# Layer 0's modulation: from reductions on VectorE to float32 products on TensorE in four groups of the array's columns

## The chip, the cores and the metric

The kernel runs on one core of one Trainium2 chip. Its time is the device time of one execution in microseconds (us), as the median of several runs. The engines are PE (TensorE), DVE (VectorE), ACT (ScalarE), POOL (GpSimd) and SP (SyncE, which here issues nearly every DMA, in one queue and in order). PEld is PE's weight load, the part of a matmul that sets the stationary operand. Each engine takes its instructions in the order in which the program has them, so an instruction that waits holds up all that stand behind it on its engine.

## The reference

Two blocks follow each other. The first takes 512 tokens of width 1024 through a gated delta rule and a dilated attention, both fed by projections of the normed input, and a gated feed-forward network. The second has two layers with a stream of 512 tokens and one of 256 context tokens; layer 0 has the "even" mixer (neighbourhood attention and differential attention), layer 1 the "odd" one (grouped attention and a long convolution, the filter of which comes from a small network with sines). Each layer of the second block is modulated:

```python
for layer in range(DEPTH_2):
    mod_l = (silu(c) @ w_ada[layer] + b_ada[layer])[:, None, :]
    mod_c = silu(c_ctx) @ w_ada[layer] + b_ada[layer]
    sh1_l, sc1_l, g1_l, sh2_l, sc2_l, g2_l = split(mod_l, 6, axis=-1)
    ...
    h_l = modulate(x_l, sh1_l, sc1_l)        # rms_norm(x) * (1 + scale) + shift
    h_c = modulate(x_c, sh1_c, sc1_c)
    ...                                      # mixer, then the same with sh2, sc2, g2 for the feed-forward
```

c and c_ctx are single vectors of 1024; w_ada[layer] is 1024 x 6144 in float32 (24 MB). So a layer's modulation is two vectors times one matrix, 2 x 6144 numbers, and each weight is used twice. It does not depend on x: it can be computed at any time before its use. The first third (shift and scale of the mixer's input) is wanted when layer 0 begins, the rest when the mixer's output is added and in the feed-forward.

## The kernel before

**Matmuls in three products.** The big projections take their weights in 512 KB chunks (`wchunk`, L305 to L315). A chunk is loaded to `wraw` by SP (two buffers), ACT rounds it to `whi` (L311), POOL takes the difference `wlo` (L312); there are three buffers of each. Activations are split in the same way, and `mm3` (L321) adds three products: hi by hi, hi by lo, lo by hi (L323, L324, L325). A matmul that is not written so, with plain float32 operands, takes PE two instruction records.

**The order.** The program is written as straight Python; a scheduler fixes at compile time the order of the instructions on each engine, with its own model of how long each takes. `issue_after` forces an instruction behind another one.

**Stage A, from the start to 130 us: projections of the delta rule.** Chunks of `w_qkv` feed PE; DVE scales each product tile (`cv_x`, L535), ACT copies it with a tap of the short convolution (`cv_y`, L537), DVE adds the other taps, ACT and DVE form the SiLU (`cv_t`). ACT also makes `whi`, in the same queue.

**Stage B, from 130.7 to 228.8 us: dilated attention's projections.** Eight chunks of `w_qk` (192 matmuls, `dq`, `dk`) and four of `w_v` (96 matmuls, `dv`, L890). In between PE runs small float32 products of the filter's network (`hyena_mlp`, L1867: `fz`, `fh` by `fw`), each followed by a sine made of six DVE instructions (`fn`, `fa`), and the row of biases (`oh`, `rl`, L868). Then the recurrence and the attention begin with transposes (`ps_p`, `ps_a`).

**Stage C, from 896.0 to 1137.7 us: layer 0's in-projection.** 24 chunks of `we_in`: six jobs of four chunks, each job 512 output columns for six tiles of 128 tokens (4 of x, 2 of the context), 144 matmuls a job, 864 in all. A job holds six PSUM banks, three called `ps_m` and three `ps_mx`, until its last chunk. For the jobs of queries and keys ACT squares and copies each tile (`qk_sq` L1364, `qk_raw` L1365, which frees the bank), DVE sums the squares (`qk_ssq` L1366), then DVE and POOL norm and rotate (L1389 to L1401), and PE transposes the result (`ps_t`, L1414) among the next job's matmuls. Stage C ends with the first scores (`ps_s`, L1571).

**The modulation.** `ada` (L1074) works on DVE. It loads both vectors to all 128 partitions (`ada_c`, 1 MB), makes the SiLU with ACT's tanh (L1084) and four DVE instructions (L1085), and then loads the transposed weights in tiles of 128 outputs by 512 inputs (`ada_w`, 256 KB, three buffers, L1091). Per tile two DVE instructions (L1093, one for each vector) multiply and sum along the row, each followed by a short read of the sum (`ada_p`). A third of a layer takes 64 of these instructions; L1099 to L1103 add the halves and the bias. `ada` is a generator: one step is 128 outputs (two loads, four reductions). `beside` and `tick` (L1107 to L1123) take some steps at every weight chunk: layer 0's first third at four steps a tick in stage B, its other two thirds at three a tick in stage C, layer 1's at 0.8 a tick in a later stage, and what is left at the end of the stage. The steps go behind DVE's latest instruction, or, in stage B, behind a fixed mark.

Of the kernel before, what the change touches and what calls it, by code (L numbers as in the profile page):

```python
# [10 lines left out]
F32 = mybir.dt.float32  # L11
# [7 lines left out]
P = 128  # L19
# [14 lines left out]
# ------------------------------------------------------------------ constants of shapes  # L34
# [90 lines left out]
# ------------------------------------------------------------------ layout of the weights  # L125
# [5 lines left out]
def _tm(w, c=512):  # L131
    """[columns / c][k / (1024 / c) / 128] chunks of [P, 1024 / c of 128 k, c columns]."""
    k, n = w.shape
    i = CH // c
    return np.ascontiguousarray(
        w.reshape(k // (i * P), i, P, n // c, c).transpose(3, 0, 2, 1, 4)
    ).reshape(n // c, k // (i * P), P, CH)
# [11 lines left out]
def layout(inp):  # L149
# [14 lines left out]
    o["w2_ada"] = np.ascontiguousarray(a["w_ada_2"].transpose(0, 2, 1)).reshape(2, 48, P, D)  # L164
# [52 lines left out]
# ------------------------------------------------------------------ the program  # L217
def kept_first(kept):
    """The tiles of an output, those with weights in kept first."""
    return list(kept) + [m for m in range(KD) if m not in kept]  # L220


class Prog:
    def __init__(self, ctx, tc, A, out, dbg=None):
# [17 lines left out]
        # an early activation: the load of its table is done by the time that data arrives  # L242
# [32 lines left out]
    # -------------------------------------------------------------- small pieces  # L275
# [14 lines left out]
    def rsqrt(self, pool, v, n, tag):  # L290
        """1/sqrt of v [P, n]."""
# [35 lines left out]
    def fm_tile(self, ps, w, act, k0, nk, m=P, off=0, first=True, last=True):  # L327
        """ps[m, t] = sum over k of w[k, m]^T act[k, t]; w: (hi, lo) chunks, act: list of (hi, lo) per k."""
# [6 lines left out]
    def after(self, ins):  # L335
        """Within, the instructions of ins's engine are queued behind it."""
        return self.tc.issue_after(ins.ins)

    def begin_proj(self, ps, tag, w_out, act, half, ms=range(3)):
        """The first tiles of an out-projection, as far as one half of act goes."""  # L340
# [6 lines left out]
    def out_proj(self, ps, w_out, act, late, n, done, begun=None):  # L347
        """done(i, m, product with the weights of tile m), i counting; the half `late` of act comes last; -> the weights
        that are still there."""
# [11 lines left out]
    @staticmethod  # L361
    def recent(ws):
        """The last of ws in the order of their loads that have not been overwritten since."""
        return dict(list(ws.items())[-3:])

    def tm_group(self, ps, tag, src, acts, done, hooks=None, order=None, behind=(), ticks=(1, 2, 3)):
        """For every tile of tokens t: ps = sum over k of act[k, t]^T w[k, columns], then done(t, ps).
        src: the chunks of w; acts: a list over t of (list over k of (hi, lo), slice of tokens); order: pairs of a chunk
        and its tiles; hooks[i]() comes after the i-th of them; behind[j, t]: what chunk j of tile t waits for;
        ticks: the chunks that count for self.beside."""  # L370
# [24 lines left out]
    def tiles_of(self, *hs):  # L395
        """The tiles of 128 tokens of split activations, for tm_group."""
# [9 lines left out]
    def token_rstd(self, pool, pspool, accs, nt, tag, div=D):  # L406
        """accs: [P, nt*128] sums of squares over one partition's features -> rstd [P tokens, nt]."""
# [21 lines left out]
    def bcast(self, ps, col, n=P):  # L429
        """ps[m, t] = col[t] for all m."""  # L430
# [8 lines left out]
    def lastb(ap, n):  # L439
        """[P, a] -> [P, a, n], each element repeated."""  # L440
# [3 lines left out]
    def midb(ap, n):  # L444
        """[P, a] -> [P, n, a], the row repeated."""
        return ap.rearrange("p (o a) -> p o a", o=1).to_broadcast([ap.shape[0], n, ap.shape[1]])

    # -------------------------------------------------------------- first block
    def block1_mixer(self, hp, psd):
        V, S, G, PE, Q, A = self.V, self.S, self.G, self.PE, self.Q, self.A  # L450
        h = hp.tile([P, 2, KD, T], F32R, name="h", tag="hx")
        with self.pools(p1=1) as (pp,):
            rb = pp.tile([P, T], F32, name="rb")
            with self.pools(g0=1) as (gp,):
                es = ExitStack()
                self.banks = {"mm": 4, "g": 4, "p": 3, "c": 1, "o": 1, "a": 2, "pv": 1}
                with self.pools(psA=1) as (ps,):
                    act = self.acts(h, 0, T)
                    da = self.pool(es, "da")
                    with self.pools(ad=1, gp1=1) as (ad, gt), ExitStack() as xs:  # L460
# [26 lines left out]
                        with self.beside(self.ada(ad, [(0, 0)]), 4, 0, self.mark):  # L487
# [20 lines left out]
    def sqacc(self, pool, acc, src, k, n=KD, eng=None, bufs=None):  # L508
        """Adds src^2 to acc, but for the last of the n parts; -> what the sum consists of."""
# [10 lines left out]
    def gdn(self, gp, gt, ps, rb, stats, act, tiles, first):  # L520
        """Projections of the gated delta rule: normed q, k, v and the gates, tokens on partitions; stats() sets rb,
        the 1 / rms of the tokens, and returns it as columns."""
# [71 lines left out]
    def gdn_gates(self, gp, gt, ps, rb, act):  # L594
        """Decay and beta, tokens on partitions."""
# [60 lines left out]
    def together(gens, beside=(), period=1):  # L656
        """Advance the generators in turn until all of gens are done, and one step of beside with each period-th round."""
# [28 lines left out]
    def gdn_prep(self, gt, ps, t, wide, out):  # L686
        """What the recurrence over the chunks of tile t needs. Products of the chunks of a head [64, 64] lie below each
        other in 64 columns or on the diagonal of 128, in wide with zeros elsewhere."""
# [26 lines left out]
        def chunkwise(a, b):  # L715
            """a^T b of the chunks of each head."""
# [6 lines left out]
        def level(lv):  # L723
            """What joins the blocks of 2^lv: A^T between the two of a pair."""
# [8 lines left out]
        # decay, transposed: exp(gc_i - gc_j) on i >= j  # L733
# [8 lines left out]
        # (I + A)^-1 and its transpose by doubling blocks: T' = T - T A_s T  # L742
# [47 lines left out]
    def gdn_chain(self, gt, ps, tag, om, t, pre):  # L790
        """The recurrence over the two chunks of tile t, the norm and the gate of its output."""
# [41 lines left out]
        # output norm and gate  # L833
# [22 lines left out]
    def dilated_bias(self, ps):  # L856
        """Per head a row of biases over 511 - distance, with the logarithm of how many patterns hold it."""
# [34 lines left out]
    def exp_rows(self, pool, src, n, bias=None, width=T, r=None, bufs=2):  # L892
        """exp(src + bias - its row maximum) and 1 / its row sum."""
# [70 lines left out]
    def finish_pair(self, pool, prb, pv, rr, dst, nt=4):  # L964
        """Divide the two heads' rows of pv by their sums and split."""
# [9 lines left out]
    def block1_tail(self, hp, ps, om, begun, x, hc):  # L975
        """x: the residual stream, to be filled; hc: the next layer's input of the context."""
# [1080 lines left out]
```

## Time and profile before

| what | value |
| --- | --- |
| time, median of 3 runs | 2716.71 us (2715.36 to 2717.19) |
| profiled execution, first to last instruction (span) | 2708.6 us |
| median less span | 8.1 us |
| PE busy | 2582.3 us, 95% |
| DVE busy | 1636.8 us, 60% |
| POOL, ACT busy | 1187.8 us (44%), 981.1 us (36%) |
| mean granted clock of PE | 0.972 |
| DMA | 257.94 MB, 95 GB/s |

The busy shares are means over the whole span. PE is busy for 95% of it, but the three stages above have idle time of PE, and DVE is the busiest engine in some of their stretches. The page prints the granted clock in tenths of full speed: 1.00 is the 2.4 GHz level and 0.50 would be a stretch wholly at the 1.2 GHz level. In the tables of waits and lines, "idle before" is the time for which the engine had nothing to run, and the name behind the arrow is what came last.

### The profile page before, as it was taken

The page shows a single profiled execution, that of the slowest core. Times are in us where ns is not written, and L with a number is a line of the kernel's source. Part 1 is how long each engine was busy: PE and PEld are TensorE (multiplying, and loading weights), DVE is VectorE, ACT ScalarE, POOL GpSimd, SP SyncE. Part 2 cuts the span into 40 slices and gives each one's busy share as a digit, 9 for nine tenths or more (in the row PEclk, how much of TensorE's full clock was granted, in tenths as well). Part 3 has the DMA queues.
Part 4 walks back from the last instruction along what each step waited for, and adds up shares of the span by engine and source line. Part 5 has one row for each costly group of instructions (what it writes and reads, how often), then busy time and mean ns, then how long its engine had stood idle before and what let it go on. Part 6 is the DMA issues. An engine that isn't in the chain of part 4 may idle for free.

```text
span 2708.6 us, 35291 instructions
## 1 busy us (share of the span) xinstructions
PE 2582.3 (95%) x13312; PEld 2093.1 (77%) x13312; DVE 1636.8 (60%) x2896; ACT 981.1 (36%) x1727; POOL 1187.8 (44%) x827
## 2 busy tenths in 40 slices
PE   8878999999999978999999999999999999999999
PEld 6667776788888757666788888888878778788887
DVE  6987546634434798776547677767576445634333
ACT  4514434322224323375524222122244543333232
POOL 3346525555556434676514232323245215444443
PEclk9989989999999989898999999999999999999999
DMA  5251112232333244301022343424242003233333
GB/s 198 81 182 46 31 55 94 86 100 88 99 102 124 98 155 139 110 17 28 28 102 86 111 134 111 138 93 149 76 136 75 20 24 124 87 95 96 104 95 94
DMA packets 103453, 257.94 MB, mean 95 GB/s; under 512 B 11745, under 2 KB 20065, under 8 KB 102900
## 3 DMA queue, kind: packets, MB, share of 16 engines
q1 hardware_dynamic: 102708, 254.64, 29.2%
q8 instruction: 105, 1.72, 0.3%
q10 hardware_dynamic: 576, 1.05, 0.1%
q14 instruction: 64, 0.52, 0.1%
HBM read 246.06 MB, written 14.83 MB: 96 GB/s over the span
## 4 chain that ended last, share of the span: by engine, by line
PE 76%; DVE 15%; DMA 3%; issue 2%; POOL 1%; ACT 1%; SPq 0%; POOLq 0%; DVEq 0%; ACTq 0%
PE ps_mm L323 13%; PE ps_mm L325 13%; PE ps_mm L324 13%; PE ps_s L1571 5%; PE ps_mx L324 3%; PE ps_mx L325 3%; PE ps_mx L323 3%; PE ps_m L324 3%; PE ps_m L323 3%; PE ps_m L325 3%; PE ps_t L435 3%; DVE ada_j L1093 2%; PE ps_pv L1702 2%; DVE ada_w L1093 2%; DMA ada_w<-in_w_ada 2%
## 5 line engine op out<-in xcount | busy, mean ns | idle before, releaser
L312 POOL TENSOR_TENSOR wlo<-wraw,whi 128x1024 fp32r<-128x1024 f32 (+2 forms) x344 | 776.3, 2260 | 1116.5 <-ACT whi L311 1034.8
L311 ACT ACTIVATE whi<-wraw 128x1024 fp32r<-128x1024 f32 (+2 forms) x345 | 336.8, 978 | 968.4 <-PE ps_mm L324 479.1
L323 PE MATMUL ps_mm<-h,whi 128*128 128x512 f32 (+1 forms) x1496 | 540.7, 363 | 11.8 <-ACT whi L311 7.3
L325 PE MATMUL ps_mm<-h,wlo 128*128 128x512 f32 (+1 forms) x1496 | 539.5, 362 | 2.3 <-POOL wlo L312 2.3
L324 PE MATMUL ps_mm<-h,whi 128*128 128x512 f32 (+1 forms) x1496 | 539.4, 362 | 1.2 <-DVE h L1145 1.0
L323 PEld LDWEIGHTS ps_mm<-h,whi 128*128 128x128 f32 x1496 | 282.4, 189 | 57.1 <-ACT whi L311 7.3
L325 PEld LDWEIGHTS ps_mm<-h,wlo 128*128 128x128 f32 x1496 | 282.0, 189 | 48.9 <-POOL wlo L312 2.9
L324 PEld LDWEIGHTS ps_mm<-h,whi 128*128 128x128 f32 x1496 | 282.2, 189 | 47.4 <-issue 1.7
L1093 DVE CUSTOM_DVE_ANT_0 ada_j<-ada_w,ada_c 128x512 f32<-128x512 f32 x192 | 195.9, 1020 | 14.7 <-DMA ada_w<-in_w_ada 14.2
L1093 DVE CUSTOM_DVE_ANT_0 ada_w<-ada_w,ada_c 128x512 f32<-128x512 f32 x192 | 186.2, 970 | 4.0
L325 PE MATMUL ps_mm<-fa,wlo 128*128 128x512 f32 (+1 forms) x528 | 186.3, 356 | 1.4 <-POOL wlo L312 1.4
L324 PE MATMUL ps_mm<-fa,whi 128*128 128x512 f32 (+1 forms) x528 | 187.6, 356 | 0.0
L323 PE MATMUL ps_mm<-fa,whi 128*128 128x512 f32 (+1 forms) x528 | 185.7, 356 | 0.0
L1270 DVE SCALAR_TENSOR_TENSOR cb<-ps_mm,small,cb 128x511 f32<-128x511 f32 (+1 forms) x66 | 43.6, 660 | 188.8 <-ACT cb L1268 188.8
L1218 DVE SCALAR_TENSOR_TENSOR x<-ps_mm,mod,x 128x512 f32<-128x512 f32 x80 | 59.4, 748 | 138.4 <-PE ps_mm L325 131.4
L903 DVE TENSOR_REDUCE nm<-ps_s 128x1 f32<-128x768 f32 (+1 forms) x96 | 74.6, 777 | 63.6 <-PE ps_s L1571 63.0
L325 PEld LDWEIGHTS ps_mm<-fa,wlo 128*128 128x128 f32 x528 | 99.0, 188 | 18.0 <-POOL wlo L312 2.0
L324 PEld LDWEIGHTS ps_mm<-fa,whi 128*128 128x128 f32 x528 | 99.2, 188 | 16.0
L323 PEld LDWEIGHTS ps_mm<-fa,whi 128*128 128x128 f32 x528 | 98.9, 188 | 16.4 <-ACT whi L311 0.3
L324 PE MATMUL ps_mx<-h,whi 128*128 128x512 f32 x216 | 86.1, 399 | 3.0 <-DVE h L1005 3.0
L323 PE MATMUL ps_mx<-h,whi 128*128 128x512 f32 x216 | 85.8, 399 | 0.5 <-ACT whi L311 0.5
L325 PE MATMUL ps_mx<-h,wlo 128*128 128x512 f32 x216 | 85.7, 397 | 0.0
(490 smaller groups left out, 5234.5 us busy)
## 6 DMA issues: line engine op xcount, KB each, us to landing
ada_w<-in_w_ada SPq DMA_DIRECT2D x192, 256.0 KB
wraw<-in_w_up SPq DMA_DIRECT2D x88, 512.0 KB
wraw<-in_w_d SPq DMA_DIRECT2D x48, 384.0 KB
wraw<-in_w_d SPq DMA_DIRECT2D x53, 320.0 KB
wraw<-in_we_in SPq DMA_DIRECT2D x24, 512.0 KB
wraw<-in_w_g SPq DMA_DIRECT2D x22, 512.0 KB
wraw<-in_w_u SPq DMA_DIRECT2D x22, 512.0 KB
wraw<-in_we_out SPq DMA_DIRECT2D x13, 512.0 KB
```

The source lines that it names most:

```text
L311: self.S.activation(hi[:, :n], raw[:, :n], AF.Copy)
L312: (eng or self.G).tensor_tensor(out=lo[:, :n], in0=raw[:, :n], in1=hi.bitcast(F32)[:, :n], op=ALU.subtract)
L323: mm(ps, lhi, rhi, start=start, stop=False)
L324: mm(ps, lhi, rlo, start=False, stop=False)
L325: mm(ps, llo, rhi, start=False, stop=stop)
L435: last = self.PE.transpose(ps[:, j * P:(j + 1) * P], src[:, j * P:(j + 1) * P], self.ident)
L903: V.tensor_reduce(out=m, in_=src, op=ALU.max, axis=AX.X, negate=True)
L1093: V.tensor_tensor_reduce(out=(junk, w)[s], in0=w, in1=c[:, s, i * T:i * T + T], scale=0.5, scalar=0.0, op0=ALU.mult, op1=ALU.add, accum_ou ...
L1218: V.scalar_tensor_tensor(out=xs[s][:, m], in0=p[:, :w], scalar=mod[:, gate * 8 + m, s:s + 1], in1=xs[s][:, m], op0=ALU.mult, op1=ALU.add)
L1270: V.scalar_tensor_tensor(out=cb[:, t0 + 1:t1], in0=pg[s][:, :w_ - 1], scalar=fw[0], in1=cb[:, t0 + 1:t1], op0=ALU.mult, op1=ALU.add)
L1571: self.PE.matmul(p[:, c0:min(n, c0 + 512)], q[i], k[i][:, c], start=i == 0, stop=i == 1)
L1702: PE.matmul(st["v"][hs, t * P:(t + 1) * P], vals(e, kt), st["t", t, e][:, kt * P:(kt + 1) * P], start=kt == 0, stop=kt == nk - 1)
```

## The change

Layer 0's modulation moves to a new function, `ada_mm`; layer 1's stays on DVE as it was. The weights of layer 0 get a layout of their own (12 blocks of 512 outputs, four 512 KB loads each, inputs on partitions), and c and c_ctx come as an 8 KB table of columns.

A block of 512 outputs goes as follows. Four loads `am_w`, three buffers. Eight float32 matmuls, one for each 128 of the inputs: the stationary operand `am_c` is 128 x 32 (two columns hold the vectors, 30 are zeros), the moving one 128 x 512 weights, and the output 32 partitions of one PSUM bank, at 32 times k mod 4, so that consecutive matmuls use different groups of 32 columns of the array, and each group sums two of the eight products. ACT copies the bank to `am_p`. After a yield, four small matmuls multiply each 128 x 128 part of `am_p` by `am_s` (128 x 2, which adds up the four groups and turns the result so that outputs lie on partitions), and one DVE instruction adds the bias and writes `mods[0]`.

Blocks 0 to 3 (the first third) run beside stage B, half a step a tick; blocks 4 to 11 beside stage C, 0.7 steps a tick. In both a step of `ada_mm` takes its PSUM banks from the ring of the stage ("g" in B, "mm" in C).

```diff
@@ layout of the weights @@
-    o["w2_ada"] = np.ascontiguousarray(a["w_ada_2"].transpose(0, 2, 1)).reshape(2, 48, P, D)
+    o["w2_ada"] = np.ascontiguousarray(a["w_ada_2"][1].T).reshape(48, P, D)
+    o["w2_ada0"] = np.ascontiguousarray(
+        a["w_ada_2"][0].reshape(4, 2, P, 12, T).transpose(3, 0, 2, 1, 4)).reshape(12, 4, P, CH)
+    o["c_col"] = np.ascontiguousarray(
+        np.stack([a["c_2"].reshape(-1), a["c_ctx_2"].reshape(-1)], 1).reshape(KD, P, 2).transpose(1, 0, 2)
+    ).reshape(P, 16)
@@ block1_mixer @@
-                        with self.beside(self.ada(ad, [(0, 0)]), 4, 0, self.mark):
+                        with self.beside(self.ada_mm(ad, ps, "g", range(4)), 0.5):
@@ new @@
+    def ada_mm(self, pool, ps, tag, blocks):
+        V, S, Q, PE, A = self.V, self.S, self.Q, self.PE, self.A
+        raw = pool.tile([P, 16], F32, name="am_r")
+        Q.dma_start(raw, A["c_col"])
+        c = pool.tile([P, KD, 32], F32, name="am_c")
+        self.G.memset(c, 0.0)
+        th = pool.tile([P, 16], F32, name="am_t")
+        S.activation(th, raw, AF.Tanh, scale=0.5)
+        V.scalar_tensor_tensor(out=th, in0=th, scalar=1.0, in1=raw, op0=ALU.add, op1=ALU.mult)
+        V.tensor_scalar(out=c[:, :, 0:2], in0=th.rearrange("p (k s) -> p k s", s=2), scalar1=0.5, scalar2=None,
+                        op0=ALU.mult)
+        sel = pool.tile([P, 2], F32, name="am_s")
+        V.tensor_reduce(out=sel, in_=self.ident.rearrange("p (j r) -> p r j", j=4)[:, 0:2], op=ALU.add, axis=AX.X)
+        for n in blocks:
+            p = self.bank(ps, tag)
+            for h in range(4):
+                w = pool.tile([P, CH], F32, name="am_w", bufs=3)
+                Q.dma_start(w, A["w2_ada0"][n, h])
+                for i in range(2):
+                    k = 2 * h + i
+                    r = 32 * (k % 4)
+                    PE.matmul(p[r:r + 32], c[:, k], w[:, i * T:(i + 1) * T], start=k < 4, stop=k >= 4)
+            part = pool.tile([P, T], F32, name="am_p", bufs=2)
+            S.activation(part, p, AF.Copy)
+            yield
+            p = self.bank(ps, tag)
+            for i in range(4):
+                PE.matmul(p[:, 2 * i:2 * i + 2], part[:, i * P:(i + 1) * P], sel, start=True, stop=True)
+            V.scalar_tensor_tensor(out=self.mods[0][:, 4 * n:4 * n + 4, :],
+                                   in0=p[:, 0:8].rearrange("p (a b) -> p a b", b=2),
+                                   scalar=float(n // 2 in (1, 4)), in1=self.lastb(self.vec("b_ada", 4 * n, 4), 2),
+                                   op0=ALU.add, op1=ALU.add)
+        yield
@@ ada @@
-                    Q.dma_start(w, A["w2_ada"][layer, grp * 16 + b, :, i * T:i * T + T])
+                    Q.dma_start(w, A["w2_ada"][grp * 16 + b, :, i * T:i * T + T])
@@ even_mixer @@
-                with self.pools(ad2=1) as (ad,), self.beside(self.ada(ad, [(0, 1), (0, 2)]), 3):
+                with self.pools(ad2=1) as (ad,), self.beside(self.ada_mm(ad, ps, "mm", range(4, 12)), 0.7):
...
```

The scheduler's order changes with it, in three places that matter below. First ACT in stage A, where the first products come out of `ps_mm`, before:

```order
20 L482 ACTIVATE rb<-ps_g 128x512
21 L311 ACTIVATE whi<-wraw 128x1024
22 L537 ACTIVATE cv_y<-cv_x,small 128x512 x2
23 L311 ACTIVATE whi<-wraw 128x1024
24 L542 ACTIVATE cv_t<-cv_y 128x512 x2
```

and after the change (lines below the new code stand some numbers lower in the file):

```order
20 L487 ACTIVATE rb<-ps_g 128x512
21 L542 ACTIVATE cv_y<-cv_x,small 128x512 x2
22 L316 ACTIVATE whi<-wraw 128x1024 x2
23 L547 ACTIVATE cv_t<-cv_y 128x512 x2
24 L316 ACTIVATE whi<-wraw 128x1024
```

The rounding of a weight chunk (`whi`) that stood ahead of the two copies `cv_y` now stands behind them.

Second PE at the end of stage B, where the last matmuls of `dv` are followed by the first scores (`ps_a` from `qd`, `ql`) and transposes, before:

```order
712 L323 MATMUL ps_mm<-whi,h 128x512
713 L324 MATMUL ps_mm<-wlo,h 128x512
714 L325 MATMUL ps_mm<-whi,h 128x512
715 L1571 MATMUL ps_a<-wraw,qd 128x128
716 L1571 MATMUL ps_a<-wraw,ql 128x128
717 L435 MATMUL ps_p<-ident,gdn_143 128x128 x8
```

and after:

```order
718 L328 MATMUL ps_mm<-whi,h 128x512
719 L329 MATMUL ps_mm<-wlo,h 128x512
720 L330 MATMUL ps_mm<-whi,h 128x512
721 L1108 MATMUL ps_g<-am_s,am_p 128x2 x4
722 L1102 MATMUL ps_g<-am_w,am_c 32x512 x8
723 L1108 MATMUL ps_g<-am_s,am_p 128x2 x4
724 L1102 MATMUL ps_g<-am_w,am_c 32x512 x8
725 L1108 MATMUL ps_g<-am_s,am_p 128x2 x4
726 L1612 MATMUL ps_a<-wraw,qd 128x128
727 L1612 MATMUL ps_a<-wraw,ql 128x128
728 L440 MATMUL ps_p<-ident,gdn_143 128x128 x8
```

Two whole blocks of `ada_mm` stand between the two. The other two blocks stand among the matmuls ahead, as six and two `am_w` matmuls with 26 others in between, twice.

Third PE in stage C, at the border of the second and the third job, before (the last tile of one, the first of the next):

```order
3191 L323 MATMUL ps_m<-whi,h 128x512
3192 L324 MATMUL ps_m<-wlo,h 128x512
3193 L325 MATMUL ps_m<-whi,h 128x512
3194 L323 MATMUL ps_mx<-whi,h 128x512
3195 L324 MATMUL ps_mx<-wlo,h 128x512
```

and after:

```order
3206 L329 MATMUL ps_m<-wlo,h 128x512
3207 L330 MATMUL ps_m<-whi,h 128x512
3208 L1102 MATMUL ps_mx<-am_w,am_c 32x512 x8
3209 L1108 MATMUL ps_m<-am_s,am_p 128x2 x4
3210 L328 MATMUL ps_m<-whi,h 128x512
```

A whole block stands at the border. A second one follows as four pairs within the first chunk or two of the new job, 2 to 26 matmuls apart. The next two borders look the same, with the four small matmuls of the earlier block ahead of the eight; the last two blocks come as six, four, two, two and two around the border of the fifth and sixth job.

## Rows read from the trace of the kernel before

**Rows 1.** the page, busy time, share of the span, instructions
```profile
PE 2582.3 (95%) x13312; PEld 2093.1 (77%) x13312; DVE 1636.8 (60%) x2896; ACT 981.1 (36%) x1727; POOL 1187.8 (44%) x827
```

**Rows 2.** the page, the chain that ended last, by engine
```profile
PE 76%; DVE 15%; DMA 3%; issue 2%; POOL 1%; ACT 1%; SPq 0%; POOLq 0%; DVEq 0%; ACTq 0%
```

**Rows 3.** reductions of the modulation: min/median/max ns, first and last start
```profile
L1093 DVE CUSTOM_DVE_ANT_0 ada_j<-ada_w,ada_c x192: 672/685/3998, 132.7 to 1934.5; 128x512 f32<-128x512 f32 x192
```

**Rows 4.** waits of ACT in stage A: us in total, times, longest
```profile
ACT whi L311 <- DMA wraw<-in_w_qkv: 11.3, 2, 5.7
```

**Rows 5.** the same of DVE
```profile
DVE cv_y L539 <- ACT cv_y L537: 6.7, 3, 6.0
```

**Rows 6.** the same of PE
```profile
PE ps_g L605 <- DVE t L602: 5.3, 1, 5.3
```

**Rows 7.** stages B, C: length; busy PE, PEld, DVE, ACT, POOL; PEclk, DMA share
```profile
130.70:228.80 98.10, 77.53 (x304) 58.56 (x304) 90.75 (x183) 24.34 (x33) 43.24 (x27) 0.88 0.50 164
896.00:1137.70 241.70, 209.37 (x925) 169.67 (x925) 206.08 (x365) 79.73 (x134) 116.72 (x57) 0.94 0.40 131
```

**Rows 8.** waits of PE in stage B
```profile
PE ps_g L1867 <- DMA fw<-in_hy_w: 9.7, 1, 9.7
PE ps_p L435 <- ACT dv L890: 6.5, 1, 6.5
PE ps_mm L323 <- DVE dk L888: 3.2, 1, 3.2
```

**Rows 9.** windows of 10 us of stage B
```profile
160.00:170.00 10.00, 9.02 (x25) 6.04 (x26) 9.72 (x21) 2.12 (x2) 2.42 (x2) 0.65 0.86 289
...
200.00:210.00 10.00, 10.00 (x33) 7.14 (x32) 9.93 (x23) 2.64 (x3) 3.71 (x3) 0.77 0.48 166
...
220.00:230.00 10.00, 3.49 (x17) 2.85 (x17) 8.97 (x27) 3.55 (x5) 2.81 (x4) 0.75 0.26 80
```

**Rows 10.** PE in time (start, us): one column half, both halves
```profile
255.44 1.09 PE L954 MATMUL ps_pv<-PT,dv 128*64 128x128 f32 x8
256.46 0.33 PE L435 MATMUL ps_a<-ident,E 128*128 128x128 f32 x1
...
259.01 1.09 PE L431 MATMUL ps_a<-ident,rr 128*64 128x128 f32 x16
260.04 0.33 PE L435 MATMUL ps_a<-ident,E 128*128 128x128 f32 x1
```

**Rows 11.** PE in time, a float32 matmul of 512 columns
```profile
434.55 1.12 PE L1900 MATMUL ps_t<-fw,fhid 64*128 64x512 f32 x2
435.60 0.50 PE L325 MATMUL ps_m<-h,wlo 128*128 128x512 f32 x1
```

**Rows 12.** PE in time, four small float32 matmuls (eight records)
```profile
22.51 0.95 PE L412 MATMUL ps_g<-ones,acc 128*128 128x1 f32 x8
```

**Rows 13.** a piece of the chain: a load of 512 KB
```profile
925.45 3.00 DMA wraw<-in_we_in
```

**Rows 14.** ACT's copies out of PSUM, by source line
```profile
L1365 ACT ACTIVATE qk_raw<-ps_mx x12: 591/603/676, 914.6 to 1063.4; 128x512 f32<-128x512 f32 x12
```

**Rows 15.** waits of PE in stage C
```profile
PE ps_mx L323 <- ACT qk_raw L1365: 18.9, 3, 9.5
PE ps_t L1414 <- DVE qk_raw L1401: 10.2, 3, 4.3
```

**Rows 16.** DVE's groups in stage C: busy us, mean ns, idle before
```profile
L1093 DVE CUSTOM_DVE_ANT_0 ada_w<-ada_w,ada_c 128x512 f32<-128x512 f32 x64 | 65.2, 1019 | 1.4
L1093 DVE CUSTOM_DVE_ANT_0 ada_j<-ada_w,ada_c 128x512 f32<-128x512 f32 x64 | 60.6, 947 | 6.2 <-DMA ada_w<-in_w_ada 6.0
L1366 DVE TENSOR_REDUCE qk_ssq<-qk_sq 128x8 f32<-128x512 f32 x24 | 16.2, 680 | 10.8 <-ACT qk_sq L1364 10.8
```

**Rows 17.** windows of stage C with a lower granted clock
```profile
950.00:970.00 20.00, 10.10 (x39) 7.64 (x38) 18.43 (x48) 8.22 (x21) 2.38 (x1) 0.81 0.67 221
...
1000.00:1020.00 20.00, 8.54 (x33) 6.36 (x32) 17.13 (x46) 7.55 (x15) 2.39 (x1) 0.75 0.60 197
```

## The prediction

> **What bounds the kernel now.** I began with the page. PE is busy for 95% of the span, DVE for 60% [rows 1], and the chain that ended last runs over PE for 76% and over DVE for 15% [rows 2]. So work given to PE costs its full length wherever PE has no gap, and DVE's work costs something only where PE waits for it. The list of reductions tells where layer 0's modulation stands: one takes 0.685 us at the median, up to 4 us [rows 3], and its places are stages B and C. The windows of these stages show the room: B is 98.1 us long with PE busy for 77.5 and DVE for 90.8; C is 241.7 long with PE busy for 209.4 and DVE for 206.1 [rows 7]. That is 20.6 and 32.3 us of idle PE, and the lists of waits say what ended it: in B a load behind others (9.7), the copy of `dv` (6.5) and `dk` on DVE (3.2) [rows 8]; in C mostly ACT's `qk_raw`, which frees the banks (18.9), and the rotated `qk_raw` from DVE (10.2) [rows 15]. ACT's wait in C is DVE's again, since DVE runs 128 reductions there, 125.8 us of busy time [rows 16]. A gap costs twice: behind it the granted clock is lower. Where the windows say 0.65, 0.77 and 0.75, PE lost 9.02 x 0.35 + 10.0 x 0.23 + 3.49 x 0.25 = 6.4 us in B [rows 9], and 10.1 x 0.19 + 8.54 x 0.25 = 4.0 us in C [rows 17]. At the full clock PE's own work is thus 77.5 - 6.4 = 71.1 us in B and 209.4 - 4.0 = 205.4 us in C.
>
> **Prices.** A float32 matmul of 512 columns takes 434.55 to 435.60, so 1.05 us [rows 11]. 96 of them one by one would be 101 us, the price if the column groups did nothing. Here is what speaks for them: eight records that go to one half of the array's columns take 1.02 us, 0.128 each, and sixteen that take the two halves by turns 1.03 us, 0.064 each [rows 10]. Two groups run side by side. Four are not in this trace, so the price of eight lies between 8.4 (one by one), 4.2 (two) and 2.1 us (four). I take two side by side for the pairs, whose groups are always two, and four where six or four stand together and all their weights are there. The Trainium skill (TensorE: Matmul & The Clock Gate, Part 3: Packing small matmuls) reports a factor of 2.38 for three column tiles of 32; by that an estimate for 96 matmuls in threes is 96 x 1.05 / 2.38 = 42 us, near the 50 of pairs, but no run here shows three.
>
> Entering and leaving the narrow shape costs nothing visible: the eight records between two 128-column ones have the price of a full-width record [rows 10]. The Trainium skill speaks against the change here (TensorEngine Tiling, Key Properties): changing the tiling mode drains TensorE. The change has some 25 such pieces. The rows just named leave room for about 0.1 us each, which would be 2.5 us; the sum doesn't hold it.
>
> Four small matmuls cost 0.95 us [rows 12]. Copying a bank takes ACT 0.60 us [rows 14], and with the hand-overs before and behind it I count 1.0 us where PE waits for it. A 512 KB load lands 3.0 us after its issue [rows 13].
>
> **Stage A.** Nothing of the change is here but the start of the queues, yet the scheduler's order on ACT differs: the two copies `cv_y` go ahead of a `whi`. That `whi` waits for its chunk (5.7 us at the longest [rows 4]), DVE's `cv_y` behind it waits for 6.0 us [rows 5], and PE later for 5.3 us [rows 6]. Since PE's wait is the later echo of DVE's, the most that can go is 6.0; something less is likely, as DVE has other work that then ends last. I take -4.5. The other end is +1, because the chunk itself is issued somewhat later behind three 512 KB loads instead of a 1 MB one.
>
> **Stage B.** Removed: 64 reductions, off DVE. Added on PE: 32 matmuls as 16 pairs, 16 x 1.05 = 16.8 us; 16 small ones, 4 x 0.95 = 3.8. The two blocks at the stage's end have eight matmuls in a row with three buffers: the fourth load can only be issued when the first pair is done (1.05), and lands at about 4.4 (3.0 and SP's issue of 0.3 on top), while three pairs end at 3.15; so 1.2 us of waiting each, 2.5. Behind each, the small matmuls wait for the copy, 2 x 1.0. Sum 25.1. The old waits: the load `fw` no longer stands behind `ada_w` loads, `dk` finds DVE free, and `dv` is copied while PE has the two blocks. With all of them gone the stage takes 71.1 + 25.1 = 96.2, which is -1.9. The bounds: -8.5 if the tail's waits vanish and four run together throughout, +9 if half of the old idle time (20.6) stays.
>
> **Stage C.** Removed: 128 reductions. Added: 64 matmuls, 32 x 1.05 = 33.6; 32 small ones, 8 x 0.95 = 7.6; at three borders a whole block, each with a late fourth load (3 x 1.2 = 3.6) and a wait for the copy (3 x 1.0). Sum 47.8. Behind such a wait stand, on PE, the next job's matmuls, and on SP three weight chunks, for the fourth load holds up SP's queue until PE has consumed a buffer; they are wanted at 36 matmuls (8 us) and more after the border, so I charge nothing. The waits for `qk_raw` go, as DVE has little left; I leave 3.0 us for the rotation, a serial piece of DVE and POOL. So 205.4 + 47.8 + 3.0 = 256.2, which is +14.5. Bounds: +5 (copies and fourth loads hidden, no old wait) and +65 (one by one).
>
> **Sum.** -4.5 - 1.9 + 14.5 = +8.1 us with two side by side. In the three sixes and the one four, four side by side save about 1.05 each, 4.2: +3.9. The remaining stages keep their work; layer 1's reductions are as before. The profiled span of 2708.6 becomes 2712.5; the median lies 8.1 above the span, so 2720.6, say **2721 us**.
>
> **Rivals.**
> 1. *The matmuls run one by one.* For it: four groups in the float32 form are nowhere in the trace; against: two groups are [rows 10]. Each of 48 pairs costs another 1.05 (50.4), less the six that the late loads give back: 8.1 + 50.4 - 6 = +52.5, 2769 us.
> 2. *PE stands at the block borders.* Slower, though the groups work: five times eight matmuls need four loads with three buffers, and the fourth is issued while weight chunks are loading too. If a load then takes 6 us instead of 3, each of the five blocks waits 3 us longer: 15 us, 2736 us. It decides from a landing time of about 4 us on. For it: in the old stage B one load held PE for 9.7 us [rows 8], and the clock fell behind it [rows 9]; against: the DMA share of stage C is 0.40 [rows 7].
> 3. *The relief of DVE is worth more.* The fourth loads and copies fall into gaps, stage A gives all 6.0, B -8.5, C +6: -8.5, 2708 us. For it: DVE is busy for 90.8 of 98.1 us in B, and a reduction can take 4 us instead of 0.7 [rows 3, 7]; against: PE has only 32.3 us of idle time and 4.0 of clock to give in C, and gets 41 of pure work there.
>
> **Chances.** The forecast (2712 to 2728) 0.46, rival 1 0.07, rival 2 0.18, rival 3 0.29. The forecast's own range straddles the line: no change can be told from one within 0.2%, 5.4 us, so up to 2722; of its 0.46 I count 0.30 as the same, 0.15 as slower and 0.01 as faster. Rivals 1 and 2 are slower (0.25), of rival 3 0.27 is faster and 0.02 the same. Faster 0.28, same 0.32, slower 0.40. The range from 2702 to 2746 takes in rival 2 with some of its own spread and rival 3 down to twice its gain in stage B; it leaves out rival 1.
>
> **What would show it.** In the new profile: pairs of the added matmuls at 1.05 us from start to start of what follows (2.1 for rival 1); the end of stage B near 220 us and of A some 4.5 earlier; stage C near 254 us, with PE's waits for `qk_raw` gone and five new waits for `am_w` of about 1.2 us (rival 2: above 4), and for `am_p` of about 1; a granted clock near 1.00 in the windows that had less. I am wrong if C is not over 246 us, since then the added work hid somewhere that I have not seen, or if stage A or B is no shorter than before.

## The result, and the profile after

The changed kernel takes 2741.29 us (2737.13 to 2742.49, 4 runs) against 2716.95 us (2715.36 to 2719.39, 4 runs): 24.3 us slower, a ratio of 1.0095 with a 95% interval of 1.0079 to 1.0112. Its profiled execution has a span of 2739.7 us and took 2741.56, so some 2 us lie around a span and not the 8.1 that the prediction put there. By that the profiled execution of before took some 2710.5 us: less than any of the four times here, but within what the same kernel took beside the later experiments (2702.8 to 2723.6). Between the two profiles the difference is 31.1 us.

The stages, from the starts of their first rows on PE (A ends with the first `oh` matmul, B with the first transpose of the recurrence, C runs from its first projection matmul to the first scores `ps_s`; the prediction's windows of B and C, 98.1 and 241.7 us, lie a little outside these):

| us | before | after | forecast |
| --- | --- | --- | --- |
| end of A | 132.2 | 132.6 | -4.5 |
| B | 96.6 | 102.6 | -4.0 |
| between B and C | 667.2 | 664.1 | 0 |
| C | 241.5 | 266.0 | +12.4 |
| behind C | 1571.1 | 1574.5 | 0 |

The busy line of the page after, in answer to [rows 1]:

```profile
PE 2641.8 (96%) x13600; PEld 2113.6 (77%) x13600; DVE 1445.7 (53%) x2514; ACT 983.3 (36%) x1733; POOL 1176.9 (43%) x829
```

DVE lost 191 us of work and PE got 59.5. The two stages as windows, to be read beside [rows 7]:

```profile
132.60:235.10 102.50, 93.83 (x397) 63.59 (x396) 29.85 (x42) 24.82 (x32) 37.63 (x26) 0.92 0.41 136
899.20:1165.20 266.00, 248.25 (x1117) 182.43 (x1117) 76.85 (x111) 83.31 (x141) 105.83 (x55) 0.95 0.35 116
```

PE still has 8.7 us of idle time in B and 17.8 in C, of another kind than before. First the waits of PE in B, then in C (total us, times, longest), in answer to [rows 8] and [rows 15]:

```profile
PE ps_g L1102 <- DMA am_w<-in_w_ada: 4.4, 2, 2.8
PE ps_g L1908 <- DMA fw<-in_hy_w: 2.7, 1, 2.7
PE ps_g L1108 <- ACT am_p L1104: 1.5, 2, 0.8
```

```profile
PE ps_mx L1102 <- DMA am_w<-in_w_ada: 8.3, 3, 2.9
PE ps_s L1612 <- POOL qd L1601: 7.4, 1, 7.4
...
PE ps_m L1108 <- ACT am_p L1104: 2.1, 3, 0.7
```

Of the waits shown for before only a part of the one for `fw` is left. In their place stand PE's waits for the new loads and copies, and one of 7.4 us at the first scores that the prediction doesn't have.

One border of jobs in C, as PE saw it (start, us; two records are one float32 matmul):

```profile
959.65 1.91 PE L1102 MATMUL ps_mx<-am_w,am_c 128*32 128x512 f32 x12
964.41 1.05 PE L1102 MATMUL ps_mx<-am_w,am_c 128*32 128x512 f32 x4 [2.85 <-DMA am_w<-in_w_ada]
966.16 1.79 PE L1108 MATMUL ps_m<-am_s,am_p 128*128 128x2 f32 x8 [0.70 <-ACT am_p L1104]
```

Six matmuls take 1.91 us: four side by side and then two. The fourth load is there 4.76 us after the start (4.4 was forecast), so PE waits 2.85 us for it. The small matmuls behind the wait take 1.79 instead of 0.95 us: the granted clock is 0.55 from 966.1 to 968.0, near the 1.2 GHz level, and until 973 the projection matmuls start 0.43 us apart instead of 0.23. In the tail of B the clock falls behind the first of two such waits and stays down through the second (granted clock third from the end):

```profile
210.00:220.00 10.00, 8.10 (x43) 4.69 (x41) 0.17 (x1) 3.35 (x5) 0.00 (x0) 1.00 0.39 127
220.00:230.00 10.00, 6.71 (x26) 2.40 (x28) 0.17 (x1) 0.60 (x1) 0.00 (x0) 0.61 0.62 218
230.00:240.00 10.00, 9.24 (x51) 6.87 (x53) 2.30 (x9) 5.32 (x12) 5.19 (x7) 0.54 0.00 0
```

The wait at the first scores, in time, first before, then after:

```profile
1114.15 1.48 ACT L1548 ACTIVATE ks<-qkb 128x1536 fp32r<-128x1536 f32 x1
...
1137.50 0.40 PE L1571 MATMUL ps_s<-ks,qd 128*128 128x512 f32 x1
```

```profile
1154.13 0.60 ACT L1514 ACTIVATE vb<-ps_mx 128x512 f32<-128x512 f32 x1 [0.77 <-PE ps_mx L330]
1154.63 1.48 ACT L1589 ACTIVATE ks<-qkb 128x1536 fp32r<-128x1536 f32 x1
...
1160.98 3.65 POOL L1591 TENSOR_TENSOR ks<-qkb,ks 64x768 fp32r<-64x768 f32 x2
1164.69 0.98 POOL L1601 TENSOR_TENSOR qd<-qkb,ql 64x128 fp32r<-64x128 f32 x2
1165.19 0.80 PE L1612 MATMUL ps_s<-ks,qd 128*128 128x512 f32 x1 [7.40 <-POOL qd L1601]
```

Before, ACT made this `ks` at 1114.15, more than 20 us ahead of the first scores, in the shadow of the last job. In the changed order it stands behind four of the last job's six copies `vb`, and POOL's part of it then has nothing to hide behind.

### The profile page after: what moved, and what is told of

Read it like the earlier page. It is cut to its first block, busy times and chain, and to the rows that moved or that the text cites. A ratio compares the mean times of both kernels' runs of the same rounds, so it can differ in the third digit from the quotient of the medians.

```text
span 2739.7 us, 35425 instructions
## 1 busy us (share of the span) xinstructions
PE 2641.8 (96%) x13600; PEld 2113.6 (77%) x13600; DVE 1445.7 (53%) x2514; ACT 983.3 (36%) x1733; POOL 1176.9 (43%) x829
## 3 DMA queue, kind: packets, MB, share of 16 engines
q10 hardware_dynamic: 576, 1.05, 0.1%
## 4 chain that ended last, share of the span: by engine, by line
PE 85%; DVE 8%; DMA 2%; issue 2%; ACT 1%; POOL 1%; SPq 0%; POOLq 0%; DVEq 0%; ACTq 0%
PE ps_mm L328 14%; PE ps_mm L330 14%; PE ps_mm L329 14%; PE ps_s L1612 5%; PE ps_mx L330 4%; PE ps_mx L328 4%; PE ps_mx L329 4%; PE ps_m L328 4%; PE ps_m L329 4%; PE ps_m L330 4%; PE ps_t L440 3%; PE ps_pv L1743 2%; PE ps_pv L1799 1%; PE ps_pv L1684 1%; DVE h L1186 1%
## 5 line engine op out<-in xcount | busy, mean ns | idle before, releaser
L1259 DVE SCALAR_TENSOR_TENSOR x<-ps_mm,mod,x 128x512 f32<-128x512 f32 x80 | 59.5, 748 | 138.3 <-PE ps_mm L330 131.4
L330 PEld LDWEIGHTS ps_mm<-fa,wlo 128*128 128x128 f32 x528 | 99.0, 188 | 17.8 <-POOL wlo L317 1.8
L1134 DVE CUSTOM_DVE_ANT_0 ada_j<-ada_w,ada_c 128x512 f32<-128x512 f32 x96 | 102.7, 1069 | 1.1 <-DMA ada_w<-in_w_ada 1.0
L1134 DVE CUSTOM_DVE_ANT_0 ada_w<-ada_w,ada_c 128x512 f32<-128x512 f32 x96 | 95.6, 996 | 2.4
L909 ACT ACTIVATE E<-ps_s,nm 128x768 f32<-128x768 f32 (+1 forms) x96 | 72.4, 755 | 40.3 <-DVE nm L908 35.1
```

Of the source, the lines that this page charges most:

```text
L330: mm(ps, llo, rhi, start=False, stop=stop)
L909: S.activation(e[:, :n], src, AF.Exp, bias=m, accum_out=s)
L1134: V.tensor_tensor_reduce(out=(junk, w)[s], in0=w, in1=c[:, s, i * T:i * T + T], scale=0.5, scalar=0.0, op0=ALU.mult, op1=ALU.add, accum_ou ...
L1259: V.scalar_tensor_tensor(out=xs[s][:, m], in0=p[:, :w], scalar=mod[:, gate * 8 + m, s:s + 1], in1=xs[s][:, m], op0=ALU.mult, op1=ALU.add)
```

## The experiments

Beside the experiments the kernel before was timed again, on the same chip; its medians there are 2713.4, 2714.2 and 2713.6 us. The changed kernel was timed only beside the 2716.95 above, so a difference from its 2741 can be some 3 us off.

**One part of the change at a time.** The other part goes back to `ada`:

```diff
-self.beside(self.ada_mm(ad, ps, "mm", range(4, 12)), 0.7)      # B alone on PE
+self.beside(self.ada(ad, [(0, 1), (0, 2)]), 3)
-self.beside(self.ada_mm(ad, ps, "g", range(4)), 0.5)           # C alone on PE
+self.beside(self.ada(ad, [(0, 0)]), 4, 0, self.mark)
```

> Only the first third of layer 0's modulation (stage B) is on TensorE; the other two thirds run on VectorE in stage C as before. Theory (the loss is made in stage C): 2717 to 2723 us, since stage B ended 5.5 us later in the changed kernel's profile (234.3 against 228.8) and gave 3 us back before stage C; stage C about 242 us long, with the old waits for qk_raw. Rival (half of the loss comes from stage B): 2727 to 2733 us.

> Only the last two thirds (stage C) are on TensorE; the first third is on VectorE in stage B as before. Theory (the loss is made in stage C): 2736 to 2742 us, stage C near 266 us long, with three late fourth loads of 2.8 us and 7.4 us of waiting at the first scores. Rival (half of it comes from stage B): 2727 to 2733 us.

B alone: 2731.96 us (6 runs), ratio 1.0064 (1.0045 to 1.0083). C alone: 2740.2 us (5 runs), 1.0092 (1.0076 to 1.0109), as its theory has it. The profile of C alone has stage C at 265.8 us and stage B at 97.4: stage C's loss is its own. B alone was expected at 2717 to 2723 and is 9 us above that. Its stage B takes 105.1 us, 8.5 more than before, and its stage C 240.3, as before; but behind C it takes 1583.4 us against 1571.1 with the same work. There the granted clock is lower, here the first two windows of 50 us before and with B alone:

```profile
1137.50:1187.50 50.00, 47.48 (x201) 31.16 (x199) 32.96 (x78) 33.66 (x88) 33.94 (x48) 0.86 0.06 20
1187.50:1237.50 50.00, 46.12 (x212) 31.66 (x212) 35.70 (x91) 34.50 (x97) 34.86 (x47) 0.88 0.08 22
```

```profile
1144.40:1194.40 50.00, 47.08 (x165) 29.75 (x163) 29.85 (x66) 27.88 (x71) 29.63 (x41) 0.71 0.07 21
1194.40:1244.40 50.00, 47.05 (x183) 33.73 (x182) 30.52 (x72) 27.06 (x76) 26.25 (x37) 0.67 0.08 22
```

So both stages lose by themselves. The sum of the two losses (18.6 and 26.8) is more than the whole; in the profiles 12 us of B alone's loss stand behind stage C, where the whole change loses 3.4. The mean clock of all six runs of B alone is low (0.964 to 0.969, against 0.966 to 0.973 for the kernel before beside it). Where it falls is seen in the one profiled run alone, and why is open.

**One column group for all.** Every matmul of a block writes partitions 0 to 31 (the lines of the copy and the small matmuls, which change with it, are left out here):

```diff
-r = 32 * (k % 4)
-PE.matmul(p[r:r + 32], c[:, k], w[:, i * T:(i + 1) * T], start=k < 4, stop=k >= 4)
+PE.matmul(p[0:32], c[:, k], w[:, i * T:(i + 1) * T], start=k == 0, stop=k == 7)
```

> All eight matmuls of a block go to the same 32 columns of the array (partitions 0 to 31 of the bank), which also take the sum; the copy and the small matmuls work on these 32 partitions. Theory (groups of columns work side by side): the 96 matmuls take 1.05 us each, 101 us instead of some 46, less the 12.7 us of waits for loads that they cover: 2778 to 2792 us. Rival (the groups don't work side by side, and the loss of the change is that): 2738 to 2746 us.

2784.48 us (one run), as the theory has it. The group of these matmuls in stage C (busy us, mean ns, idle before), first in the changed kernel, then with one column group:

```profile
L1102 PE MATMUL ps_mx<-am_w,am_c 128*32 128x512 f32 x128 | 28.9, 607 | 8.3 <-DMA am_w<-in_w_ada 8.3
```

```profile
L1101 PE MATMUL ps_mx<-am_w,am_c 128*32 128x512 f32 x128 | 59.9, 612 | 6.7 <-DMA am_w<-in_w_ada 6.5
```

64 matmuls take 59.9 us, 0.94 each, against 28.9 us in the changed kernel. The column groups do work side by side.

**No modulation in C.** In the kernel before, the call of `ada` in stage C goes, and constants stand for the last two thirds.

> The kernel before, but stage C has no modulation work at all: the last two thirds of layer 0's modulation are left out, and their values are constants. It shows what freeing DVE is worth when nothing is given to PE. Theory (the waits for qk_raw all come from the reductions): stage C falls from 241.5 to 206 to 212 us and the time by 28 to 36 us; the rest of the change's stage C (266 us) is then PE's price of the moved work, some 56 us. Rival (the rotation chain and the copies bound these waits anyway): stage C 222 us or more.

2675.77 us (4 runs), ratio 0.9867 (0.9849 to 0.9885). The window of its stage C:

```profile
899.10:1102.60 203.50, 200.95 (x924) 164.98 (x925) 73.00 (x100) 77.62 (x130) 109.06 (x57) 1.00 0.20 68
```

203.5 us, and PE is busy for 200.95 of them at the full clock. Both numbers are better than the theory's. Taking the reductions off DVE is thus worth 38.0 us in C when PE is given nothing, and PE's price of the moved work in the changed kernel is 266.0 - 203.5 = 62.5 us. This run also lacks the 16 MB of loads; that they don't matter here is seen in the run with other banks below, which has them and 0.5 us of idle PE in C.

**No fourth load.**

```diff
-w = pool.tile([P, CH], F32, name="am_w", bufs=3)
-Q.dma_start(w, A["w2_ada0"][n, h])
+if h < 3:
+    w = pool.tile([P, CH], F32, name="am_w", bufs=3)
+    Q.dma_start(w, A["w2_ada0"][n, h])
```

> As the changed kernel, but the fourth load of every block is left out, and the last two matmuls of a block read the third load's tile again (a quarter of the weights is left out, PE's work is the same). Theory (the fourth load is late because only three buffers exist): the five waits of 1.6 to 2.9 us (12.7 together) vanish, the clock behind them is better, and the time is 11 to 18 us below the changed kernel's 2741: 2723 to 2730. Rival (the wait is for PE's own partial results or the queue, and moves elsewhere): less than 4 us.

2710.56 us (10 runs; 0.9995 of before, 0.9978 to 1.0012): 31 us below the changed kernel, more than twice what the waits add up to and below the theory's range. Stage B takes 90.8 us, C 243.6. The added matmuls themselves are cheaper; first those of B in the changed kernel, then B and C in this run:

```profile
L1102 PE MATMUL ps_g<-am_w,am_c 128*32 128x512 f32 x64 | 14.6, 716 | 4.4 <-DMA am_w<-in_w_ada 4.4
```

```profile
L1103 PE MATMUL ps_g<-am_w,am_c 128*32 128x512 f32 x64 | 8.1, 601 | 0.0
...
L1103 PE MATMUL ps_mx<-am_w,am_c 128*32 128x512 f32 x128 | 20.4, 601 | 3.0 <-DMA am_w<-in_w_ada 3.0
```

8.1 and 20.4 us, against 14.6 and 28.9. In B eight or four now stand together and run four wide, where the changed kernel has six and two in each block, the last block at half the clock (3.77 and 1.92 us instead of 1.91 and 1.05). In C there are eights and fours among the pairs, where the changed kernel has sixes and pairs. By these rows the fourth load costs three times: the wait, the clock behind it, and matmuls that come in twos. What each is worth this run doesn't separate, since the order and a quarter of the loads change with it. Four buffers instead of three have no time: with them the pool of `ada_mm` in stage C takes 21.2 KB per partition and 17.7 are left there, so the 2724 to 2730 us that were expected of them stay unanswered. The late `ks` is still there with its 7.4 us.

**Other banks.** One word:

```diff
-self.beside(self.ada_mm(ad, ps, "mm", range(4, 12)), 0.7)
+self.beside(self.ada_mm(ad, ps, "t", range(4, 12)), 0.7)
```

> One word is changed against the changed kernel: in stage C the blocks take their PSUM banks from the ring of the transposes (ps_t) instead of the ring that a job holds. Theory (the ring forces whole blocks onto the job borders, where late loads and copies stop PE and the setup of the first scores is pushed behind the last products): in stage C the waits for am_w and am_p fall from 10.4 to under 2 us, the 7.4 us at the first scores go, stage C takes 237 to 245 us instead of 266, and the time falls by 20 to 28 us to 2713 to 2721. Rival (PE's own time for the added matmuls is the loss): stage C not under 255 us, time above 2730.

2710.29 us (12 runs), 0.9989 of before (0.9974 to 1.0004), somewhat below the theory's range. Stage C, and the matmuls of its first block:

```profile
898.70:1132.50 233.80, 233.28 (x1116) 176.04 (x1117) 87.89 (x111) 82.35 (x139) 108.28 (x58) 1.00 0.38 130
```

```profile
946.53 1.91 PE L1102 MATMUL ps_t<-am_w,am_c 128*32 128x512 f32 x12
...
954.10 1.05 PE L1102 MATMUL ps_t<-am_w,am_c 128*32 128x512 f32 x4
```

233.8 us, 32 less than in the changed kernel, with 0.5 us of idle PE and the clock at 1.00. The blocks now come as six and two with other matmuls in between, the loads are there in time, and in this order `ks` stands ahead of all six `vb`. So PE's own price of the moved work is 30 us; the other 32 of the 62.5 were made by where the blocks stood: 17 us of idle PE, 8 on the added matmuls themselves (39.2 us against 31.3) and 7 on the rest of PE's work, at a mean clock of 0.95.

**Four parts of the inputs in one load.** The layout of the weights and the loop change, so that the matmuls of one load always use all four column groups (the lines for 24 blocks and for copies and sums of 256 columns are left out here):

```diff
-            for h in range(4):
+            for h in range(2):
                 ...
-                for i in range(2):
-                    k = 2 * h + i
-                    r = 32 * (k % 4)
-                    PE.matmul(p[r:r + 32], c[:, k], w[:, i * T:(i + 1) * T], start=k < 4, stop=k >= 4)
+                for i in range(4):
+                    r = 32 * i
+                    PE.matmul(p[r:r + 32, :C], c[:, 4 * h + i], w[:, i * C:(i + 1) * C], start=h == 0, stop=h == 1)
```

It was run with the transposes' ring and with the job's ring.

> As the run with the transposes' ring, and a load holds four of the eight parts of the inputs by 256 columns instead of two by 512, so that the four matmuls of one load always use four different column groups; 24 blocks of 256 columns, two loads each, so none needs a fourth buffer. Same weights, same sums. Theory (pairs leave half of the groups idle, four groups run side by side): four matmuls of 256 columns take 0.53 us from start to end, stage B 88 to 95 us instead of 102.6, stage C 232 to 239, time 2696 to 2708, below the kernel before. Rival (two at a time is all the array does): stage B no shorter than 98 us, time as with the transposes' ring alone.

> The loads of four parts by 256 columns, but the banks in stage C from the job's ring as in the changed kernel. Theory (it is the ring that stalls stage C): stage B as in the run before (88 to 95 us), stage C 246 to 260 us with waits for am_w of 5 us and more at the borders; time 2712 to 2728. Rival (only the width matters): stage C within 4 us of the run before.

With the transposes' ring 2699.1 us (7 runs), 0.9947 of before (0.9928 to 0.9965): faster than both kernels, if only by half a per cent of before. Stage B takes 88.6 us, C 237.8, all as the theory has it. One block of it in stage B, eight matmuls of 256 columns, and the projection matmul behind:

```profile
140.24 1.07 PE L1101 MATMUL ps_g<-am_w,am_c 128*32 128x256 f32 x16
141.24 0.50 PE L328 MATMUL ps_mm<-h,whi 128*128 128x512 f32 x1
```

Eight take 1.00 us, the work of four of the old width. All of them in stage C (busy us, mean ns, idle before):

```profile
L1101 PE MATMUL ps_t<-am_w,am_c 128*32 128x256 f32 x256 | 17.4, 389 | 3.4 <-issue 3.4
```

With the job's ring it is 2734.37 us (4 runs), 1.0074 (1.0055 to 1.0093), 6 us above the expected range: stage B is as short (90.8), but C takes 264.6 us, nearly 5 more than was expected at most, with these waits:

```profile
PE ps_mx L1101 <- DMA am_w<-in_w_ada: 10.4, 9, 2.8
PE ps_s L1611 <- POOL qd L1600: 7.8, 1, 7.8
PE ps_m L1107 <- ACT am_p L1103: 5.5, 8, 1.3
```

The loads of four parts are worth some 12 to 14 us in B: the added matmuls take 8.8 us instead of 14.6 (with the transposes' ring), and the waits for `am_w` and `am_p` (4.4 and 1.5) are gone with the fourth load. In C they gain nothing: 237.8 against 233.8 with the one ring, 264.6 against 266.0 with the other. There the ring decides, though not alone: with the job's ring and without the fourth load C took 243.6. Leaving out the fourth load takes away 22 of the 32 us that the place had cost, the other ring all of them; so the loss needs both, whole blocks at the borders and loads that come late for them.

## Why the prediction came out as it did

The measured 2741 lies in the range (2702 to 2746), on the side that had the largest chance (slower, 0.40), but the sum had +3.9 us and the runs have +24.3. The range was wide enough to hold rival 2 as well, so that the time fell into it says little for the sum; and one of the prediction's own signs of being wrong came true, since neither A nor B is shorter than before. In the profiles it was short by 4.8 us in A, 10.0 in B, 12.1 in C and 3.4 behind C, and 3.1 us too high between B and C. Step by step:

- *Column groups side by side, two at 1.05 us.* Right. A pair takes 973.88 to 974.87 in the profile after, and one group for all costs 43 us more. Four wide, which no row before showed, is right too: 0.94 us one by one, 0.27 for the same width in fours (17.4 us for 128 matmuls of half the width), a factor of 3.4. The Trainium skill (TensorE: Matmul & The Clock Gate, Part 3: Packing small matmuls) has 2.38 for three column tiles. That lies between this case's 1.8 for two (two times 0.94 in 1.05) and 3.4 for four; no run here has three.
- *The change of shape at 0.1 us.* Nearly right. In the rows below the next projection matmul would have started at 973.79; the pair's successor starts at 974.87, and from there to the next it takes 0.34 instead of 0.23. That is 1.19 us, 0.14 above the pair's own price. The Trainium skill's rule (TensorEngine Tiling (Array Packing), Key Properties: changing the mode drains TensorE) fits with that. That a drain takes this time isn't shown: behind float32 transposes of the full shape the first projection matmul takes 0.31 to the next, so 0.08 of the 0.14 comes without a change of shape.

```profile
956.10 0.60 PE L1455 MATMUL ps_t<-ident,qk_raw 128*128 128x128 f32 x4
956.46 0.48 PE L330 MATMUL ps_m<-whi,h 128*128 128x512 f32 x1
956.77 0.39 PE L328 MATMUL ps_mx<-whi,h 128*128 128x512 f32 x1
...
973.56 0.40 PE L330 MATMUL ps_m<-whi,h 128*128 128x512 f32 x1
973.88 1.05 PE L1102 MATMUL ps_mx<-am_w,am_c 128*32 128x512 f32 x4
974.87 0.50 PE L328 MATMUL ps_mx<-whi,h 128*128 128x512 f32 x1
975.21 0.40 PE L329 MATMUL ps_mx<-wlo,h 128*128 128x512 f32 x1
```

- *Stage A, -4.5.* Wrong: +0.3. PE's wait of 5.3 us [rows 6] is gone, but the chain of the gates on DVE then ends last, and PE waits for it some 20 us later. The list of waits names no releaser there (`issue`); in time, DVE's `g` is what ends just before:

```profile
PE ps_g L643 <- issue: 5.1, 1, 5.1
```

```profile
68.60 0.17 DVE L639 SCALAR_TENSOR_TENSOR g<-sp_q,ea 128x16 f32<-128x16 f32 x1
```

  At this matmul, at 68.88 against 70.69 before, the changed kernel is still 1.8 us ahead; behind the wait the granted clock is 0.72 from 68 to 80 us, where before had 1.00, and the lead is lost. The prediction said that DVE's other work would end last and still took three quarters of the wait as a gain.
- *Stage B, -4.0.* Wrong: +6.0. The old waits for `dk` and `dv` went as forecast, 2.7 of the 9.7 for `fw` stayed. The tail's waits came to 4.4 + 1.5 instead of 2.5 + 2.0. The added `am_w` matmuls took 14.6 us where the sum had 14.7, but by luck: six in a row ran quicker than priced, and the last block stood at half the clock. The small ones took 5.6 instead of 3.8, also behind the waits. The sum had no term for a clock that falls behind the new waits, though [rows 9] showed it behind the old ones. The largest piece is another: for the rest of PE's work the sum had 69.6 us from 132.2 on (71.1 from 130.7), and it took 73.6, and 73.1 in the later run with 88.6 us, at a mean clock of 0.98. The sum had taken off too much for the slow clock.
- *Stage C, relief of DVE.* Mis-sized: without modulation PE's work is 201 us, not 205.4, since the slow clock had cost 8.4 and not the 4.0 of two windows. The relief is worth 38 us; the sum had 33.
- *Stage C, the fourth load at 1.2 us each.* Mis-sized: 8.3 us instead of 3.6. Its landing was nearly right (4.4 forecast, 4.8 measured), but it was set against pairs that end at 3.15; six matmuls four wide end at 1.91. The sum took the gain of four wide (4.2) as a term of its own and didn't see that where a wait follows, a quicker engine only waits longer. One part of that gain didn't come: the one four ran as two pairs, 2.08 us.
- *Stage C, the clock behind the new waits.* Not in the sum. PE's old work, 201 us at the full clock, took 209.1, and the small matmuls 10.3 instead of 7.6: some 11 us.
- *Stage C, "I charge nothing" for what stands behind.* Wrong by 7.4 us, though not at the place that was looked at (the weight chunks on SP, which were in time): the order of ACT at the end of the stage had moved, and that was not looked up.

So what failed in C is the price of the place where the blocks stand: some 23 us too little for the late load, the clock and the late `ks`. Half of that was hidden by terms that were too high: PE's old work by 4.4 us, the added matmuls by 2.6, the rotation, for which PE didn't wait at all, by 3.0, and the copies by 0.9.

Rival 1 (one by one) is excluded by the one-group run. Rival 2 had the place right, whole blocks at the borders, and a time near the measured one (2736), but not for its reason: loads didn't take longer (2.65 to 2.85 us of waiting in C, less than its 4). Rival 3 (more relief) is true of the relief and was eaten by the rest.

## What to carry to other kernels

Work moved to the engine that is busy for 95% of the time pays only if it costs less there than the waits that it removes, and the price is set by where the scheduler can put it: here 30 us in stage C with PSUM banks from the transposes' ring, 62.5 with banks from a ring that a job holds, 40 with that ring and one load less a block. A block whose inputs need more buffers than there are carries one load's latency within it, and a quicker engine makes that wait longer, not shorter. For groups of array columns, lay out the loads so that each one feeds all groups.

## What the runs showed of the hardware

The kernel before, unchanged, took from 2702.8 to 2723.6 us beside the experiments, and its time goes with the mean granted clock: 0.975 at 2702.8, 0.967 at 2723.6. Where it gains or loses this can't be seen, since only one execution of it was profiled. The stretch that differs most between kernels with the same work is the 150 us or so behind stage C, where PE has many short waits: there the kernel before shows 0.86, 0.88 and 0.89 in three windows of 50 us, B alone 0.71, 0.67 and 0.97, the run with other banks 0.86, 0.62 and 0.77. A single profile can thus be more than 10 us off the median for reasons that lie far from the change: the profiled execution of the run with other banks took 2723.8 us, its median is 2710.3.
